# A hand-written order for ScalarE around the S5 output stage: set DMAs behind the next clearing, a sign and four scaling units moved, three scratch rows renamed

## The chip, the cores and the metric

The kernel runs on one core of a Trainium2 chip. The metric is the device time of one execution in microseconds (us). Before the change it is 1008.78 us, the median of three runs (1008.59 to 1009.65). Engines are named as the profile names them: PE is TensorE's matmuls and PEld its weight loads, DVE is VectorE, ACT is ScalarE, POOL is GpSimd, SP is SyncE, which here only issues DMAs. A "q" behind a name (ACTq, SPq) is the engine's queue issuing a DMA.

## The reference

One layer over 1024 latent tokens of width 1024 with a context of 256 tokens, in float32. Depth is 1, so the mixer is the bidirectional S5 state-space model, and only the latent stream is returned.

```python
h_l = modulate(rms_norm(x, norm_mix[i]), m_l[0], m_l[1])      # m_* from SiLU(c) @ ada_w + ada_b
bu = einsum('lgh,gnh->lgn', u, b_bar)                         # 64 groups x 64 complex states, both directions
_, h = associative_scan(combine, (lam_bar, bu))               # h_l = lam_bar h_{l-1} + bu_l, context first
y  = einsum('lgn,ghn->lgh', h, c_mat).real                    # summed over both directions
g  = gelu(y + d_skip * h_l);  x = x + gate * g * sigmoid(g @ w_glu + b_glu)
x  = x + gate2 * swiglu(h2, w1, w3, w2);  out = rms_norm(x, norm_final)
```

## The kernel before, in words

**Chunks.** Tokens are cut into chunks of 8: 32 context chunks and 128 latent chunks. DVE computes the states at the chunk borders one step after another (`scan`): 32 steps of two chunks each up to the middle of the latent stream, then 56 more to its end. What lies inside a chunk is a Toeplitz product. The scan's instructions stand on DVE as one unbroken series; ACT, POOL, PE and SP work beside it on a program of their own.

**Units.** The 64 groups fall into eight units k = 0 to 7 of eight groups, two units to a quarter q = k//2. For each unit PE needs (a) the border states, with the odd chunks of the first half filled in from the even ones, (b) the matrices `CL[q]` that carry a state to the eight tokens of its chunk, and (c) the Toeplitz rows `KQ`.

**The program.** `PROG1` is a string of two-part words that `run` issues in order; each engine sees its own instructions in that order, in program order, and waits by semaphores. Letters: `A` adds more of the conditioning product (`ada`, PE, line 534, with the loads it frees, line 523); `K n` is one half of a quarter's Toeplitz set (`k_mats`: matmuls on lines 845 to 853 into the PSUM tiles `kt` and a second one, two ACT copies on line 856 into `KX`, two DMAs from ACT's queue to DRAM on line 858); `O n` clears the second tile for the next half (`zeros`, ACT copy, line 807); `T n` loads Toeplitz rows back with a shift (`toeplitz`, SP's queue, line 866; `T` number u serves unit u//2); `L` and `G` load the output matrices of a quarter and flip a sign in them (ACT, line 671), `q` sums them (POOL); `C` makes `CL` (POOL products, and for some parts a PE sum with an ACT copy, lines 693 and 694, or an accumulating DMA from POOL, line 696); `f k p` is part p of four of unit k's scaling for the odd chunks (`fill_mul`, four ACT instructions, lines 948 and 949, into a scratch tile `FT[k-2]`); `F k` adds it to the states (`fill_add`, three POOL instructions); `R k` turns the backward states of the first half round (`turned`, ACT copy, line 988, into `HSe[k]`); `P k` is the unit's state product for the first half (PE, line 1008), `X k` its Toeplitz product (PE, line 1032), `Y` the two copies of the result to SBUF (ACT, line 1093). `M` turns the conditioning rows (line 964 copies them out of PSUM).

Then `PROG2` follows: `Z` turns the second half's states (DVE or ACT by `ZEN`), `N k` is the state product of the second half (PE, line 1008 into `pe` tiles), `D` adds it (DVE), `H` the GELU (ACT), `Q 6` and `Q 7` the whole of units 6 and 7, and the GLU begins.

**What holds what.** The PSUM pool behind `P`, `O` and the PE sums has three tiles, so `P k` needs the `Y` copies of the unit before. `PROG1`'s last PSUM tiles are read by `K 7`'s copies; the pool of `PROG2` opens when these and the scan have let go. Every DMA of SP's and ACT's queues takes one of eight completion semaphores in turn, in program order, and its issue waits until the DMA that used the same semaphore before it has landed.

**Rows.** `RA` holds the states; its first 4 KB (`RA` 0 to 4) are context states that are dead after the first scan steps and serve as scratch. `RXc` 0 to 4 is a second scratch, `RC[3]` holds `CL[3]`, whose last 4 KB (12 to 16) are written only by `C33`.

Of the kernel before, what the change touches and what calls it, by code (L numbers as in the profile page):

```python
# [28 lines left out]
MAGIC = 12582912.0  # L29
HOWS = "YPYP EPEP EEEE EPYE"  # L30
ZEN = "VVSVSVSV"
PROG1 = ("A22 G1 B0 A26 A30 C01 O0 C03 q1 A34 K0 O1 L2 A38 A42 C10 C11 K1 O2 G2 A46 A50 C12 C13 f20 f21 A54 K2 O3 f22 f23 A58 T0 T1 T2 T3 q2 C20 R0 R1 K3 L3 C22 F2 A64 M0 P0 R2 f30 f31 X0 Y0 Y1 T4 T5 f32 f33 P1 X1 Y2 Y3 T6 T7 f40 f41 C21 C23 F3 P2 X2 Y4 Y5 R3 G3 M1 q3 K4 f42 f43 C30 P3 K5 X3 Y6 Y7 T8 T9 T10 T11 C31 F4 R4 f50 f51 f52 f53 C32 F5 P4 X4 R5 Y8 Y9 f60 f61 P5 X5 Y10 Y11 C33 f62 f63 K6 K7 f70 f71 f72 f73 F6 F7 T12 T13 T14 T15 w0 l1 M2 m0 w1")
PROG2 = ("Z0 N0 Z1 Z2 D0 Z3 N1 D1 Z4 H0 H1 N2 D2 H2 N3 Z5 D3 H3 N4 D4 z6 z7 I0 J0 I1 J1 H4 N5 D5 I2 J2 H5 I3 J3 W0 W1 W2 W3 x0 x1 x2 x3 Q6 H6 I4 J4 Q7 I5 J5 V1 b0 w20 w21 l1 H7 g03 g13 I6 J6 g23 g05 g15 I7 J7 V2 g26 x10 x11 x12 x13")
GAPS = (5, 6, 6, 6, 6, 6, 6, 8)
LOG2E = 1.4426950408889634
# [7 lines left out]
def s5_ffn_kernel(tc, a, out):  # L43
# [3 lines left out]
    with ctx:  # L47
        ctx.enter_context(tc.manual_schedule())
        sb = ctx.enter_context(tc.tile_pool(name="sb", bufs=1))
        def region(tag, kb, dt=F32):  # L50
            return sb.tile([P, int(kb * 256)], dt, tag=tag, name=tag)

        def view(reg, kb, shape, parts=P):
            off = int(round(kb * 256))
            n = int(np.prod(shape))
            v = reg[:parts, off:off + n]
            if len(shape) > 1:
                names = "abcdef"[:len(shape)]
                v = v.rearrange(f"p ({' '.join(names)}) -> p {' '.join(names)}",
                                **{k: d for k, d in zip(names, shape)})  # L60
            return v

        ENG = {"S": S, "V": V, "E": E}
        R0 = region("r0", 7)
        RA = region("ra", 80.5)
        RU = region("ru", 40)
        RC = [region(f"c{i}", 16) for i in range(4)]
        RXa, RXc = region("rxa", 8), region("rxc", 8)
# [49 lines left out]
        STB = 20.125  # L118
# [60 lines left out]
        def ps_(i):  # L179
            return (LTa, lbt)[i // 8][:, G * (i % 8):G * (i % 8) + G]  # L180

        def t_(i):
            return view(RA, 0.75 + 0.25 * i, [G])
# [31 lines left out]
        k2, k1, p1, dt, k4, kp, pp, sp, cs, pr, lrep, limp, r2p, snp, ta_, tb_ = [ps_(i) for i in range(16)]  # L215
        k3, r1, pw2, be, al, rp, r2, u2, pw3, sn, q1, q2, tc_, td_ = [t_(i) for i in range(14)]
# [449 lines left out]
        def cs_load(q, eng=SY):  # L666
            eng.dma_start(Cs[q][:, 0:2], a["cxy"][:, q])
# [167 lines left out]
        def bb(q, d, ri, a_):  # L835
            return BBn[q // 2][:, ri, d, 8 * (q % 2) + a_]

        def k_mats(q, hq, kts):

            tiles = [(g_, 2 * gi + hq, kts[g_][32 * gi:32 * gi + HC], slice(64 * g_, 64 * g_ + 64), (64 * g_, 32 * gi))  # L840
                     for gi in range(4) for g_ in range(2)]
            for d, c0, c1, ts_ in ((1, 128, 240, slice(7, 0, -1)), (0, 0, 112, slice(6, None, -1))):
                for ri in range(2):
                    for g_, a_, kv, ps, tp in tiles:
                        PE.matmul(kv[:, c0:c1], bb(q, d, ri, a_)[ps], CL[q][ps, ri, d, a_, ts_], start=ri == 0, stop=ri == 1,
                                  tile_position=tp)
            for g_, a_, kv, ps, tp in tiles:
                l0 = 64 * g_ + HC * (tp[1] // 32)
                PE.matmul(kv[:, 112:128], ident[ps, l0:l0 + HC], KD[ps, q, hq], start=True, stop=False, tile_position=tp)
            for d in range(2):  # L850
                for ri in range(2):
                    for g_, a_, kv, ps, tp in tiles:
                        PE.matmul(kv[:, 112:128], bb(q, d, ri, a_)[ps], Cs[q][ps, ri, d, a_], start=False,
                                  stop=d + ri == 2, tile_position=tp)
            for g_ in range(2):
                S.copy(KX[2 * hq + g_], kts[g_])
            for g_ in range(2):
                S.dma_start(KD_[q][:, 2 * hq + g_], KX[2 * hq + g_])

# [77 lines left out]
            while rest:  # L937
                one()

        FT = [view(r, kb, [2, 32, 2, 8]) for r, kb in ((RXc, 0), (RA, STB), (RXc, 0), (RXc, 0), (RA, STB), (RXc, 0))]  # L940

        def fill_mul(k, part):

            ft, e0 = FT[k - 2], 8 * (k % 2)
            st = STQ[k // 2][:, 31:95:2]
# [5 lines left out]
        def fill_add(k):  # L951

            ft, e0 = FT[k - 2], 8 * (k % 2)
            st = STQ[k // 2][:, 32:95:2, :, e0:e0 + 8]
# [79 lines left out]

        scan()
        inner, KO = {}, {}
        HSe = [view(r, kb, [64, 2, 4]) for r, kb in ((RC[3], 14), (RC[3], 12), (RC[3], 14), (RC[3], 12), (RA, 2), (RA, 0))]
        HSl = [view(RA, STB * (i // 3) + 4.125 + 2 * (i % 3), [64, 2, 4]) for i in range(6)]
        HSq = {6: view(RA, 0, [P, 2, 4]), 7: view(RA, STB, [P, 2, 4])}

        def run(prog):


            for w in prog.split():
                op, i = w[0], int(w[1:])
# [4 lines left out]
                elif op == "M":  # L1050
                    mod_cols(i)
                elif op == "K":
                    k_mats(*divmod(i, 2), [kt, KO[i] if i < 4 else pm[:, 0:15 * HC]])
                elif op == "L":
                    cs_load(i, SY if i == 3 else S)
                elif op == "G":
# [8 lines left out]
                elif op == "C":  # L1065
                    q, part = divmod(i, 10)
# [136 lines left out]
        def glu_mm(cq, s):  # L1203
# [14 lines left out]
            return pz  # L1218

        run(PROG1)  # L1220
        psW.__exit__(None, None, None)
        psA.__exit__(None, None, None)
        psE = tc.tile_pool(name="psE", bufs=1, space=bass.MemoryType.PSUM, reuse_waits="tile")
        pE = psE.__enter__()
        for _ in range(4):
            pe8([512])
        run(PROG2)
        W0, GR = W0[0], GR[0]
        X1 = region("c3", 16)
# [93 lines left out]
        for cq in range(2):  # L1323
            for s in range(4):
                k = 4 * cq + s
# [56 lines left out]
        G2 = region("c3", 16, R32)  # L1382
# [420 lines left out]
        for i, (kind, ft, j) in enumerate(seq):  # L1803
# [12 lines left out]
            if kind == "U":  # L1816
# [4 lines left out]
                if (ft, j) in LAST:  # L1821
                    k, h = LAST[ft, j]
# [63 lines left out]
```

## Time and profile before

| | |
|---|---|
| median of three runs | 1008.78 us (1008.59 to 1009.65) |
| the profiled execution, its own time | 1009.95 us |
| its span, first to last instruction | 1008.2 us |
| granted TensorE clock, mean | 0.991 |
| busy: PE, DVE, POOL, ACT | 949.6, 772.8, 746.0, 455.1 us |
| the scan's 88 steps on DVE, last instruction | ends at 216.8 us |
| `P 0`, first matmul on PE | starts at 173.66 us |
| `N 0`, first matmul on PE | starts at 225.28 us |
| from 250 to 330 us | PE busy 20.00 of each 20 us |

Times inside the run are counted from the span's first instruction. In a timeline row the first number is the start, the second the length, and in brackets stands how long the engine was idle before and what ended it. In a table of windows each engine has its busy time in the window with the number of instructions; after POOL stand the granted PE clock (1.00 is full), the mean share of the DMA engines and the GB/s. A busy PE only says that matmuls were in flight.

### The profile page before, as it was taken

What the parts mean: (1) busy time and instruction counts of PE and PEld (TensorE: products, weight loads), DVE (VectorE), ACT (ScalarE), POOL (GpSimd) and SP (SyncE); (2) the same over time, 40 slices, a digit from 0 to 9 for tenths busy, and PEclk for the clock granted to TensorE, in tenths of its full rate; (3) what the DMA queues carried; (4) which work ended last, traced back from release to release, by engine and by line L of the source; (5) the groups of instructions that cost most, each with busy time, mean ns of one, the idle gap of its engine ahead of it and who ended that gap; (6) DMA issues with size and microseconds to landing.
All of it is one profiled execution on the core that took longest, in us unless ns stands there. A gap on an engine that the chain in (4) does not pass through costs nothing. (4 is left out here: it accounts for less than half of the span.)

```text
span 1008.2 us, 17807 instructions
## 1 busy us (share of the span) xinstructions
PE 949.6 (94%) x6604; PEld 748.5 (74%) x6604; DVE 772.8 (77%) x1618; ACT 455.1 (45%) x904; POOL 746.0 (74%) x581
## 2 busy tenths in 40 slices
PE   5987798879999999999999999999999999999996
PEld 1466434758888878778888888888888888888885
DVE  8979999964456777878958677686858677686987
ACT  5488524666434563343243343434243343324337
POOL 5799999764735358979785878777785878777764
PEclk9999998999999999999999999999999999999999
DMA  9765997235521022011212120111212111111205
GB/s 336 282 135 107 298 303 263 70 79 173 180 81 36 0 105 84 12 43 42 73 45 82 42 72 24 62 53 53 73 43 84 42 54 41 54 63 53 73 21 167
DMA packets 48687, 98.39 MB, mean 98 GB/s; under 512 B 4300, under 2 KB 18892, under 8 KB 47320
## 3 DMA queue, kind: packets, MB, share of 16 engines
q1 hardware_dynamic: 43560, 86.91, 26.0%
q0 software_dynamic: 2160, 7.87, 4.2%
q10 hardware_dynamic: 2880, 2.48, 0.8%
q8 instruction: 52, 0.85, 0.3%
q14 instruction: 35, 0.29, 0.1%
HBM read 83.20 MB, written 6.17 MB: 89 GB/s over the span
## 5 line engine op out<-in xcount | busy, mean ns | idle before, releaser
L77 POOL TENSOR_TENSOR c<-rxc,c 128x512 fp32r<-128x512 f32 x127 | 166.0, 1321 | 53.7 <-ACT c L1341 52.9
L1400 PE MATMUL ut<-ra,c 128*128 128x512 f32 x400 | 155.7, 389 | 1.2 <-DVE ra L77 1.2
L1399 PE MATMUL ut<-ra,c 128*128 128x512 f32 x400 | 155.7, 389 | 0.2 <-ACT ra L1341 0.2
L1401 PE MATMUL ut<-ra,c 128*128 128x512 f32 x400 | 155.6, 389 | 0.0
L1341 ACT CAST c<-rxc 128x512 fp32r<-128x512 f32 x128 | 79.1, 622 | 146.7 <-PE xt L1694 53.3
L1694 PE MATMUL xt<-c,c 128*128 128x512 f32 x540 | 129.7, 389 | 0.0
L77 DVE TENSOR_TENSOR ru<-ru,xt 128x1024 f32<-128x1024 f32 x90 | 107.9, 1216 | 13.3 <-PE xt L1694 9.4
L1694 PEld LDWEIGHTS xt<-c,c 128*128 128x128 f32 x540 | 101.4, 188 | 21.0
L77 DVE TENSOR_TENSOR ru<-ut,ru 128x512 f32<-128x512 f32 x98 | 67.2, 686 | 42.6 <-PE ut L1401 37.2
L1400 PEld LDWEIGHTS ut<-ra,c 128*128 128x128 f32 x400 | 75.1, 188 | 17.0 <-POOL rxc L77 1.5
L1399 PEld LDWEIGHTS ut<-ra,c 128*128 128x128 f32 x400 | 75.1, 188 | 16.1 <-ACT ra L1341 0.6
L1401 PEld LDWEIGHTS ut<-ra,c 128*128 128x128 f32 x400 | 75.1, 188 | 15.6
L77 POOL TENSOR_TENSOR rxc<-rxc 128x512 f32<-128x512 f32 (+1 forms) x43 | 64.0, 1487 | 6.9 <-ACT rxc L671 5.3
L77 POOL TENSOR_TENSOR c<-ru,c 128x512 fp32r<-128x512 f32 (+1 forms) x39 | 58.7, 1505 | 10.1 <-ACT c L1341 5.7
L77 POOL TENSOR_TENSOR c<-rw,c 128x512 fp32r<-128x512 f32 (+1 forms) x28 | 37.4, 1336 | 37.3 <-ACT c L1341 37.3
L1399 PE MATMUL ut<-c,c 128*128 128x512 f32 x160 | 62.3, 390 | 0.8 <-DVE rxa L77 0.8
L1401 PE MATMUL ut<-c,c 128*128 128x512 f32 x160 | 62.3, 389 | 0.0
L1400 PE MATMUL ut<-c,c 128*128 128x512 f32 x160 | 62.2, 389 | 0.0
L1694 PE MATMUL ut<-c,c 128*128 128x512 f32 x216 | 51.9, 389 | 0.0
L77 DVE TENSOR_TENSOR ru<-ru,ut 128x512 f32<-128x512 f32 x76 | 47.3, 680 | 0.3
L1694 PEld LDWEIGHTS ut<-c,c 128*128 128x128 f32 x216 | 40.6, 188 | 8.4
L77 DVE TENSOR_TENSOR pe<-pe,ru 128x512 f32<-128x512 f32 x32 | 22.3, 696 | 30.8 <-PE pe L1217 17.1
(462 smaller groups left out, 2432.5 us busy)
## 6 DMA issues: line engine op xcount, KB each, us to landing
c<-in_ada_w SPq DMA_DIRECT2D x46, 256.0 KB, 6.5
rxc<-in_w SPq DMA_DIRECT2D x38, 256.0 KB, 2.9
rxc<-in_w SPq DMA_DIRECT2D x19, 512.0 KB
ru<-in_w SPq DMA_DIRECT2D x11, 512.0 KB
rw<-in_w SPq DMA_DIRECT2D x11, 512.0 KB, 3.6
ra<-in_ada_w SPq DMA_DIRECT2D x10, 512.0 KB, 10.7
c<-c POOLq DMA_DIRECT2D x9, 512.0 KB, 5.7
ra<-in_ada_w SPq DMA_DIRECT2D x18, 256.0 KB, 5.4
```

The costliest lines, as they stand in the source:

```text
L77: eng.tensor_tensor(out=o, in0=x, in1=y, op=op)
L1341: S.copy(o[0], x)
L1399: PE.matmul(pu, wh, bh, start=start, stop=False)
L1400: PE.matmul(pu, wh, bl, start=False, stop=False)
L1401: PE.matmul(pu, wl, bh, start=False, stop=stop)
L1694: PE.matmul(pd, w[:, cs_], b, start=j in (1, 2, 4) and n == 0, stop=n == 2, skip_group_check=j not in (1, 2, 4))
```

## The change

It adds no arithmetic and takes none away. `k_mats` no longer issues its two DMAs; a new word `k` does (`k_rows`), and it stands behind the next `O`. Word by word in `PROG1`: `G3` moves ahead of `f40`; `R2` behind `f30 f31`; unit 5's four parts move ahead of and behind `X3 Y6 Y7`; unit 6's four parts stand together behind `R4`; `Y8 Y9` go ahead of `R5`; unit 7's parts take the place of unit 6's behind `R5` and `Y11`, so none is left behind `C33`. `FT[3]` (unit 5) moves from `RXc` to `RA` 0, and `HSe[4]` from `RA` 2 to `RC[3]` 14.

```diff
-PROG1 = ("A22 G1 B0 A26 A30 C01 O0 C03 q1 A34 K0 O1 L2 A38 A42 C10 C11 K1 O2 G2 A46 A50 C12 C13 f20 f21 A54 K2 O3 f22 f23 A58 T0 T1 T2 T3 q2 C20 R0 R1 K3 L3 C22 F2 A64 M0 P0 R2 f30 f31 X0 Y0 Y1 T4 T5 f32 f33 P1 X1 Y2 Y3 T6 T7 f40 f41 C21 C23 F3 P2 X2 Y4 Y5 R3 G3 M1 q3 K4 f42 f43 C30 P3 K5 X3 Y6 Y7 T8 T9 T10 T11 C31 F4 R4 f50 f51 f52 f53 C32 F5 P4 X4 R5 Y8 Y9 f60 f61 P5 X5 Y10 Y11 C33 f62 f63 K6 K7 f70 f71 f72 f73 F6 F7 T12 T13 T14 T15 w0 l1 M2 m0 w1")
+PROG1 = ("A22 G1 B0 A26 A30 C01 O0 C03 q1 A34 K0 O1 k0 L2 A38 A42 C10 C11 K1 O2 k1 G2 A46 A50 C12 C13 f20 f21 A54 K2 O3 k2 f22 f23 A58 T0 T1 T2 T3 q2 C20 R0 R1 K3 k3 L3 C22 F2 A64 M0 P0 f30 f31 R2 X0 Y0 Y1 T4 T5 f32 f33 P1 X1 Y2 Y3 T6 T7 G3 f40 f41 C21 C23 F3 P2 X2 Y4 Y5 R3 M1 q3 K4 k4 f42 f43 C30 P3 K5 k5 f50 f51 X3 Y6 Y7 f52 f53 T8 T9 T10 T11 C31 F4 R4 f60 f61 f62 f63 C32 F5 P4 X4 Y8 Y9 R5 f70 f71 f72 P5 X5 Y10 Y11 f73 C33 K6 k6 K7 k7 F6 F7 T12 T13 T14 T15 w0 l1 M2 m0 w1")
@@ k_mats
             for g_ in range(2):
                 S.copy(KX[2 * hq + g_], kts[g_])
+
+        def k_rows(q, hq):
             for g_ in range(2):
                 S.dma_start(KD_[q][:, 2 * hq + g_], KX[2 * hq + g_])
@@ fill_mul's scratch
-        FT = [view(r, kb, [2, 32, 2, 8]) for r, kb in ((RXc, 0), (RA, STB), (RXc, 0), (RXc, 0), (RA, STB), (RXc, 0))]
+        FT = [view(r, kb, [2, 32, 2, 8]) for r, kb in ((RXc, 0), (RA, STB), (RXc, 0), (RA, 0), (RA, STB), (RXc, 0))]
@@ turned states
-        HSe = [view(r, kb, [64, 2, 4]) for r, kb in ((RC[3], 14), (RC[3], 12), (RC[3], 14), (RC[3], 12), (RA, 2), (RA, 0))]
+        HSe = [view(r, kb, [64, 2, 4]) for r, kb in ((RC[3], 14), (RC[3], 12), (RC[3], 14), (RC[3], 12), (RC[3], 14), (RA, 0))]
@@ run
                     k_mats(*divmod(i, 2), [kt, KO[i] if i < 4 else pm[:, 0:15 * HC]])
+                elif op == "k":
+                    k_rows(*divmod(i, 2))
```

The orders of PE, DVE, POOL and SP stay as they were; only ACT's rows move, and POOL's and PE's rows read other scratch. In the changed file the lines behind `k_mats` stand two further down, those behind `run`'s new branch four.

ACT at `K 2`, `O 3` and the first rows of `f22`, before and then after (`kt` and `pw` are the two PSUM tiles, `kd` the Toeplitz set in DRAM):

```order
L856 COPY r_60<-kt 128x240
L856 COPY r_60<-pw 128x240
L858 DMA kd_1255<-r_60 128x240 x2
L807 COPY pw<-r_60 128x240
L948 ACTIVATE rxc<-ra,r_60 128x64
```

```order
L856 COPY r_60<-kt 128x240
L856 COPY r_60<-pw 128x240
L807 COPY pw<-r_60 128x240
L860 DMA kd_1255<-r_60 128x240 x2
L950 ACTIVATE rxc<-ra,r_60 128x64
```

The clearing (L807) now stands ahead of the two DMAs instead of behind them.

ACT from `Y 10 Y 11` to the copies of the last Toeplitz halves, before (the eight scalings are `f62 f63`) and then after (the four are `f73`):

```order
L1093 COPY ru<-pw 128x4x8x16 x2
L948 ACTIVATE ra<-ra,r_60 128x64
L949 ACTIVATE ra<-ra,r_60 128x64
L948 ACTIVATE ra<-ra,r_60 128x64
L949 ACTIVATE ra<-ra,r_60 128x64
L948 ACTIVATE ra<-ra,r_60 128x64
L949 ACTIVATE ra<-ra,r_60 128x64
L948 ACTIVATE ra<-ra,r_60 128x64
L949 ACTIVATE ra<-ra,r_60 128x64
L856 COPY r_60<-kt 128x240
L856 COPY r_60<-pm 128x240
L858 DMA kd_1257<-r_60 128x240 x2
```

```order
L1097 COPY ru<-pw 128x4x8x16 x2
L950 ACTIVATE rxc<-ra,r_60 128x64
L951 ACTIVATE rxc<-ra,r_60 128x64
L950 ACTIVATE rxc<-ra,r_60 128x64
L951 ACTIVATE rxc<-ra,r_60 128x64
L856 COPY r_60<-kt 128x240
L856 COPY r_60<-pm 128x240
L860 DMA kd_1257<-r_60 128x240 x2
L856 COPY rw<-kt 128x240
L856 COPY rw<-pm 128x240
L860 DMA kd_1257<-rw 128x240 x2
L990 COPY ra<-ra 128x512 x2
```

Behind the last DMAs the second half's turned states (`Z 2`, `Z 4`, L990 in the changed file, L988 before) now follow at once; before, sixteen scalings of unit 7 stood between.

ACT at the fourth sign, before (behind `Y 4 Y 5` and `R 3`) and after (behind `Y 2 Y 3`):

```order
L1093 COPY ru<-pw 128x4x8x16 x2
L988 COPY c_66<-ra 128x512
L671 ACTIVATE rxc<-rxc 128x256
L972 COPY r_60<-pw 128x4x4 x2
L856 COPY r_60<-kt 128x240
```

```order
L1097 COPY ru<-pw 128x4x8x16 x2
L671 ACTIVATE rxc<-rxc 128x256
L950 ACTIVATE rxc<-ra,r_60 128x64
L951 ACTIVATE rxc<-ra,r_60 128x64
L950 ACTIVATE rxc<-ra,r_60 128x64
```

The sign flip (L671) now stands ahead of `f40 f41` (eight scalings), `Y 4 Y 5` and `R 3`, which were ahead of it.

## The prediction

> **What bounds the kernel now.** I read the windows by stage first, to see where PE, which is in flight 94% of the span, is not. Columns: PE, PEld, DVE, ACT, POOL busy with their counts, PE clock, DMA share, GB/s.
>
> ```profile
> 210.00:230.00 20.00, 13.62 (x483) 12.43 (x487) 8.72 (x43) 11.97 (x37) 9.43 (x8) 0.91 0.14 36
> 230.00:250.00 20.00, 18.84 (x452) 18.00 (x448) 10.39 (x18) 14.24 (x22) 9.44 (x12) 1.00 0.61 186
> 250.00:270.00 20.00, 20.00 (x210) 17.23 (x210) 8.53 (x7) 5.45 (x8) 13.18 (x7) 1.00 0.54 175
> ```
>
> PE lacks 6.4 us between 210 and 230 and 1.2 in the next 20; from 250 on it is full. Whatever brings PE's full stretch forward brings the end forward. So the timeline says which wait ends last there:
>
> ```profile
> 211.84 0.49 PE L1008 MATMUL pw<-c,ra 64*64 64x128 f32 x2 [2.34 <-POOL ra L77]
> 213.65 3.02 PE L1008 MATMUL pw<-c,ra 64*64 64x128 f32 x62 [1.33 <-ACT ru L1093]
> 222.88 0.36 PE L845 MATMUL kt<-c,rxa 64*16 64x112 f32 x2 [1.89 <-ACT r L856]
> 225.28 1.31 PE L1008 MATMUL pe<-c,ra 64*64 64x128 f32 x33 [0.47 <-ACT rw L856]
> 227.45 3.33 PE L1008 MATMUL pe<-c,ra 64*64 64x128 f32 x99 [0.86 <-issue]
> 231.93 4.35 PE L1008 MATMUL pe<-c,ra 64*64 64x128 f32 x131 [1.16 <-ACT ra L988]
> 216.78 0.76 DVE L990 COPY ra<-ra 128x512 f32<-128x512 f32 x2
> 228.82 1.29 DVE L77 TENSOR_TENSOR ru<-pe,ru 128x512 f32<-128x512 f32 x2 [11.27 <-PE pe L1008]
> ```
>
> These are `P 5` (two rows), `K 7`, `N 0`, `N 1`, `N 2`; then DVE's turned states `Z 0 Z 1`, right behind the scan. DVE is done with the scan at 216.78 and then idles 11.27 us for PE. So the scan is not the bound: `N 0` could start at 217.2 (half of the 0.76) and starts at 225.28. Those **8.1 us are the most** that an earlier `N 0` can give; the 1.16 us ahead of `N 2` (ACT's `Z 2`) come on top. PE is held by ACT, directly or through POOL:
>
> ```profile
> 204.60 0.61 ACT L988 COPY ra<-ra 128x512 f32<-128x512 f32 x1
> 209.54 0.40 ACT L949 ACTIVATE rxc<-ra,r 128x64 f32<-128x64 f32 x1
> 212.50 0.62 ACT L988 COPY ra<-ra 128x512 f32<-128x512 f32 x1 [2.56 <-POOL ra L77]
> 213.02 1.07 ACT L1093 COPY ru<-pw 128x512 f32<-128x512 f32 x2
> 219.19 1.07 ACT L1093 COPY ru<-pw 128x512 f32<-128x512 f32 x2 [2.72 <-PE pw L1032]
> 222.49 0.34 ACT L856 COPY r<-kt 128x240 f32<-128x240 f32 x1
> 225.25 1.22 ACTq L858 DMA_DIRECT2D kd<-rw  x2
> 231.28 1.12 ACT L988 COPY ra<-ra 128x512 f32<-128x512 f32 x2
> 209.74 2.73 POOL L77 TENSOR_TENSOR ra<-ra,rxc 128x512 f32<-128x512 f32 x3 [2.35 <-ACT rxc L948]
> 214.53 2.39 POOL L77 TENSOR_TENSOR c<-c,rw 128x1024 f32<-128x1024 f32 x1
> ```
>
> From `R 4` (ends 205.2) to the last of unit 5's sixteen scalings (ends 209.94) a scaling costs 0.30 us. Then POOL adds (`F 5`, 209.74), ACT turns (`R 5`, 212.50), copies `Y 8 Y 9` (213.02), and only then PE gets the bulk of `P 5`. Behind `Y 10 Y 11` (219.19) eight more scalings hold `K 6`'s copies until 222.49, and sixteen more hold `Z 2` until 231.28.
>
> **The change, part by part.**
>
> *The sets' DMAs behind the clearing.* Three of the four clearings were not waited for by PE. The fourth was:
>
> ```profile
> 166.38 0.97 ACTq L858 DMA_DIRECT2D kd<-r  x2
> 167.39 0.36 ACT L807 COPY pw<-r 128x240 f32<-128x240 f32 x1 [3.42 <-DMA c<-in_ada_w]
> 167.81 0.36 PE L845 MATMUL pw<-c,c 64*16 64x112 f32 x1 [3.26 <-ACT pw L807]
> 168.00:170.00 2.00, 2.00 (x139) 1.97 (x125) 2.00 (x13) 2.00 (x8) 1.50 (x2) 0.50 0.62 165
> 173.66 0.39 PE L1008 MATMUL pw<-c,ra 64*64 64x128 f32 x2
> 164.26 0.80 SPq L523 DMA_DIRECT2D ra<-in_ada_w  x2
> ra<-in_ada_w SPq DMA_DIRECT2D x10, 256.0 KB, 5.0
> 170.06 1.13 ACT L988 COPY c<-ra 128x512 f32<-128x512 f32 x2
> 173.81 0.59 ACT L964 COPY ra<-pm 128x512 f32<-128x512 f32 x1 [2.11 <-PE pm L534]
> ```
>
> `K 2`'s copies end at 167.39 − 3.42 = 163.97; the DMAs then wait for a semaphore that an `in_ada_w` load still holds, and `O 3` with `K 3` waits behind them. PE idles 3.26 us and comes back at half clock (0.50 in 168 to 170), so `K 3` and `A 64` last until 173.7 and `P 0` starts at 173.66. Now `O 3` runs at 163.9 and `K 3` from 164.3 to 166.0 (1.7 us: `K 6` runs from `X 5`'s end near 219.3 to 222.88 − 1.89). `A 64` waits for its last load, issued at 164.7 and 5.0 us on its way: done near 170.0. The DMAs still hold `f22` until 167.4 instead of 167.7, so `R 0`, which stood at 170.06, comes at 169.75 and `P 0`'s bulk at **170.3: 3.3 us earlier**. `k0`, `k1`, `k3` cost nothing: ACT issues the same two DMAs one 0.36 us copy later, and their readers `T` go out microseconds later (below).
>
> *The middle of the program.* A `P` costs 2.3 and an `X` 2.05 us at full clock:
>
> ```profile
> 177.40 7.00 SPq L866 DMA_DIRECT2D ra<-kd  x4
> 205.26 2.26 PE L1008 MATMUL pw<-c,ra 64*64 64x128 f32 x60 [0.77 <-ACT ra L988]
> 175.86 2.05 PE L1032 MATMUL pw<-ra,ru 128*128 128x128 f32 x16
> 178.92 1.05 ACT L1093 COPY ru<-pw 128x512 f32<-128x512 f32 x2
> 196.77 0.17 PE L853 MATMUL pm<-rw,rxa 64*16 64x16 f32 x1 [1.92 <-issue]
> 196.93 3.13 PE L1032 MATMUL pw<-ra,ru 128*128 128x128 f32 x16
> 199.66 1.07 ACT L1093 COPY ru<-pw 128x512 f32<-128x512 f32 x2 [2.02 <-PE pw L1032]
> 198.00:200.00 2.00, 2.00 (x11) 2.00 (x11) 2.00 (x13) 0.34 (x1) 2.00 (x2) 0.50 0.38 123
> ```
>
> `X 0` ends at 174.7. ACT meanwhile does `K 3`'s copies, `M 0` (172.0; `A 64` no longer holds it to 173.81), `f30 f31` (2.4) and `R 2` (0.5), and reaches `Y 0` at 175.4, not 178.92. `R 2` behind `f30 f31` waits for nothing: `P 0`, whose row it reuses, is over. `P 1` needs `Y 0`: `X 1` ends at 180.2, `P 2` and `X 2` at 185 (their `T` loads go out from 177.40 on, as before), `K 4` at 187.4, `P 3` at 189.8, `K 5` with the 1.92 us stall that the profile puts down to nothing at 193.4, `X 3` at 3.13 (half clock again) at 196.6. Unit 5's first two parts (2.4) stand ahead of `Y 6` now, behind `K 5`'s copies and DMAs: ACT is free at 197.2, so `Y 6` comes at 197.2, not 199.66, 0.6 later than it could. Next `f52 f53` 2.4, two PE-sum copies and `R 4` at 201.6, not 204.60. **3.0 of the 3.3 us survive.**
>
> *The sign.*
>
> ```profile
> 189.78 0.43 ACT L671 ACTIVATE rxc<-rxc 128x256 f32<-128x256 f32 x1
> 190.29 0.73 POOL L77 TENSOR_TENSOR rxc<-rxc 128x256 f32<-128x256 f32 x1 [5.35 <-ACT rxc L671]
> ```
>
> POOL idles 5.35 us for `G 3`. Behind `Y 2 Y 3` it comes near 181.3; POOL is then still in `C 23` and `F 3` (free at 190.29 − 5.35 = 184.94), so POOL's whole series moves forward by 5.3. Alone that is worth nothing to PE, since `F 5` waits for ACT (2.35). It pays with the next part, as `F 5` then finds POOL free.
>
> *Unit 5 in other rows, earlier; units 6 and 7 earlier.* Unit 5's scratch in `RA` 0 lets it start without waiting for `F 4` to leave `RXc`. Its last scaling ends at 200.6 instead of 209.94; `F 5` (2.73) runs behind POOL's `C 32`, which ends 206.50 + 0.88 − 5.3 before and so near 202, until 204.8. `P 4` and `X 4` after `R 4` end at 206.5. Unit 6's sixteen (4.7) stand behind `R 4` and end at 206.9: **`Y 8` at 206.9 instead of 213.02, `R 5` at 208.0 instead of 212.50, the bulk of `P 5` at 208.5 instead of 213.65: 5.2 us.** `X 5` ends 4.3 us on (full clock) or 5.8 (3.02 + 2.8, as in the trace): 212.8 to 214.3. `Y 10 Y 11` and four scalings of unit 7 (1.07 + 1.2) put `K 6`'s copies at 215.1 to 216.6 instead of 222.49. From them to `N 0` it is 225.28 − 222.49 = 2.8: **`N 0` at 217.9 to 219.4**, 0.7 behind the scan's floor or more.
>
> `HSe[4]` in `RC[3]` makes `C 33`'s product wait for `P 4` (204.4). `C 33` takes 4.5 (to 216.92 in the trace, from 212.4), so it ends near 209.3; `K 6` needs it at 212.8. The cover is 3.5 us; only what `P 4` loses beyond would cost. `F 6` and `F 7` end before 220 on an idle POOL.
>
> *Behind `N 0`.* ACT issues `k7`'s DMAs (1.22) and does `Z 2` at once, so `N 2` follows `N 1`: 5.5 us after `N 0` (230.78 − 225.28), at 223.4 to 224.9 instead of 231.93. **Sum: 7.0 to 8.5 us; I take 7.8.** `T12` to `T15` and the GLU's loads stand on SP's queue behind `k7` and move with it by 6 to 7 us, and PE needs `T12` only at `Q 6`, so they stay hidden; all later work hangs on PE.
>
> The profiled execution took 1009.95, 1.17 above the median of the runs: 1002.2 for one like it and **1001.0 us** against 1008.78.
>
> [...]
>
> **The rivals.** *The first 3.3 us are lost* (20%): the loads of `A 64` come later, or PE idles in pieces between them and stays at half clock through `P 0` and `X 0`, as in 168 to 170. For it: PE has only six matmuls between 166 and 170. Then `Y 6` comes at 200.7, later than before, behind `f50 f51`; `R 4` 205.2, `Y 8` 210.4, `P 5` 212.1, `N 0` 221.5 to 223.0, `N 2` 227.0 to 228.5: 4.2 us, 1004.6.
>
> *Nothing at the end* (5%): a load or POOL takes PE's place behind `N 0` and 1008.8 stays. Against it: PE's 20.00 of 20 from 250, with DMA at 0.54 of its time.
>
> *Slower* (5%): PE's rows of small matmuls are fed no faster than now. The gaps of 1.92 and 0.86 with "issue" behind them stand in such rows, and the change packs `K 3`, `K 4`, `K 6` and `K 7` closer. A stall costs 1.92, and 1.08 for the half clock behind it (3.13 − 2.05): 3.0. Two leave a gain; from three on (9.0 against 7.8) it is slower: 1010.0. Against it: `K 6` and `N 2` to `Q 7` run as dense as that without one.
>
> **How the numbers follow.** The forecast has 68%, with its own range 999.4 (8.5 and the 0.86 gap gone) to 1002.6; 2% lie below. The range for 8 in 10 takes in most of the first rival: 999.0 to 1005.0. Below 0.2% (2 us) a measurement of this kernel cannot be told from no change; so faster 0.90, same 0.05, slower 0.05.
>
> **What would show it.** Right: `K 3`'s first matmul near 164.3 with no half clock behind it; `P 0` near 170.3; POOL's sum of the fourth sign near 185; `F 5` with no wait for ACT; `N 0` near 218 and DVE's idle ahead of it down from 11.27 to some 4 us; no wait ahead of `N 2`; the span after 250 as long as before. Wrong: an `N 0` beyond 222, new "issue" gaps, or PE idle behind 250 that was not there.

## The result, and the profile after

The changed kernel takes 1003.34 us (median of five runs, 1001.83 to 1006.10), the kernel before 1009.44 (1008.59 to 1011.98): ratio 0.9939, 95% interval 0.9916 to 0.9962, so 6.1 us faster and at least 3.8. The profiled execution of the changed kernel took 1001.83 us, with a span of 1000.0 against 1008.2 before. The executions of either kernel lie 3 to 4 us apart here and up to 7 us in the later runs; how that bears on the numbers is taken up below.

The windows of the profile after, by stage, with the columns of the table before:

```profile
210.00:230.00 20.00, 17.67 (x670) 16.63 (x664) 14.37 (x54) 12.14 (x27) 6.14 (x9) 1.00 0.34 88
230.00:250.00 20.00, 20.00 (x394) 18.56 (x389) 8.03 (x12) 8.79 (x14) 11.62 (x10) 1.00 0.44 154
250.00:270.00 20.00, 20.00 (x100) 16.50 (x99) 9.15 (x10) 9.14 (x13) 14.93 (x7) 1.00 0.66 224
```

PE had 13.62 and 18.84 us busy in the first two windows; it has 17.67 and 20.00 now, 5.2 us more, and the clock in the first is 1.00 where it was 0.91. The timeline shows the same steps as before the change, some now in other rows. PE first (`P 5` in two rows, `K 7`, the first 33 matmuls of `N 0`, and the rest of `N 0` with everything up to the GELU's first transposes as one row), then DVE, ACT and POOL:

```profile
208.25 0.48 PE L1010 MATMUL pw<-c,ra 64*64 64x128 f32 x2 [0.58 <-ACT ru L1097]
209.25 2.25 PE L1010 MATMUL pw<-c,ra 64*64 64x128 f32 x60 [0.52 <-ACT ra L990]
217.36 0.25 PE L845 MATMUL kt<-c,rxa 64*16 64x112 f32 x1 [0.42 <-issue]
218.92 1.31 PE L1010 MATMUL pe<-c,ra 64*64 64x128 f32 x33 [0.47 <-ACT rw L856]
220.93 9.28 PE L1010 MATMUL pe<-c,ra 64*64 64x128 f32 x287 [0.70 <-issue]
217.24 1.32 DVE L992 COPY ra<-ra 128x512 f32<-128x512 f32 x2
222.30 1.29 DVE L77 TENSOR_TENSOR ru<-pe,ru 128x512 f32<-128x512 f32 x2 [3.75 <-PE pe L1010]
207.63 1.04 ACT L1097 COPY ru<-pw 128x512 f32<-128x512 f32 x2
208.57 0.62 ACT L990 COPY ra<-ra 128x512 f32<-128x512 f32 x1
215.43 0.35 ACT L856 COPY r<-kt 128x240 f32<-128x240 f32 x1
219.99 1.14 ACT L990 COPY ra<-ra 128x512 f32<-128x512 f32 x2 [0.86 <-ACT rw L856]
184.35 0.73 POOL L77 TENSOR_TENSOR rxc<-rxc 128x256 f32<-128x256 f32 x1
201.22 3.08 POOL L77 TENSOR_TENSOR ra<-ra 128x512 f32<-128x512 f32 x3
205.42 2.03 POOL L77 TENSOR_TENSOR c<-rxc,rxa 128x1024 f32<-128x1024 f32 x1 [1.12 <-PE pw L1010]
```

`N 0` starts at 218.92 instead of 225.28, DVE's idle ahead of `D 0` is 3.75 us instead of 11.27, and no row stands between 220.93 and 230.21 in which PE waits, so the 1.16 us ahead of `N 2` are gone. The 0.70 us with "issue" stand inside `N 0`, as the 0.86 us did before: a state product has 64 matmuls, and the row ahead of the gap holds 33 of them. The prediction, and the expectations of e3 and e9, put that gap into `N 1`; it lies in `N 0`, so `D 0` waits for it. At the front, `O 3` runs ahead of the two DMAs, but `K 3` has a gap of its own:

```profile
162.84 0.38 ACT L807 COPY pw<-r 128x240 f32<-128x240 f32 x1
164.59 1.40 ACTq L860 DMA_DIRECT2D kd<-r  x2
166.03 0.41 ACT L950 ACTIVATE rxc<-ra,r 128x64 f32<-128x64 f32 x1 [2.81 <-DMA c<-in_ada_w]
167.11 0.19 PE L853 MATMUL kt<-rxc,c 64*16 64x16 f32 x1 [2.48 <-issue]
193.57 0.18 PE L853 MATMUL pm<-rw,rxa 64*16 64x16 f32 x1 [2.46 <-issue]
193.75 3.78 PE L1034 MATMUL pw<-ra,ru 128*128 128x128 f32 x16
```

The clearing no longer waits; the DMAs and the scalings behind them do. PE's two gaps of 2.5 us with "issue" behind them, in `K 3` and in `K 5`, are what the rest of the study turns on.

### The profile page after: what moved, and what is told of

Its sections match the earlier page's. It is cut to its first block, busy times and chain, and to the rows that moved or that the text cites. A ratio compares the mean times of both kernels' runs of the same rounds, so it can differ in the third digit from the quotient of the medians.

```text
span 1000.0 us, 17808 instructions
## 1 busy us (share of the span) xinstructions
PE 949.0 (95%) x6604; PEld 749.1 (75%) x6604; DVE 772.9 (77%) x1618; ACT 454.7 (45%) x904; POOL 746.3 (75%) x581
## 3 DMA queue, kind: packets, MB, share of 16 engines
q10 hardware_dynamic: 2880, 2.48, 0.8%
```

## The experiments

**A clock for comparing single profiles.** Executions of one kernel differ by up to 2.6 us before the first moved word is reached: `bb_turn` (L827), which stands ahead of all of them, starts at 127.75 in the first profile of the changed kernel and at 130.34 in its second. The second and third profiles are e4 and e11 for the changed kernel, e8 and e12 for the kernel before. So I count from the start of DVE's `Z 0`, which follows the scan at once and waits for nothing else, to `D 0`, DVE's first addition behind `N 0`, and from there to the end. Both are rows of DVE's timeline; the first two here are of the changed kernel's third profile, the last two of the third profile of the kernel before:

```profile
217.28 0.76 DVE L992 COPY ra<-ra 128x512 f32<-128x512 f32 x2
220.98 1.29 DVE L77 TENSOR_TENSOR ru<-pe,ru 128x512 f32<-128x512 f32 x2 [2.94 <-PE pe L1010]
```

```profile
217.08 0.76 DVE L990 COPY ra<-ra 128x512 f32<-128x512 f32 x2
228.00 1.29 DVE L77 TENSOR_TENSOR ru<-pe,ru 128x512 f32<-128x512 f32 x2 [10.16 <-PE pe L1008]
```

All profiles, read in this way (us; the last two columns are the timed runs against the kernel before, on the same chip):

| kernel | Z 0 starts | Z 0 to D 0 | D 0 to end | ratio | interval |
|---|---|---|---|---|---|
| before | 216.8, 217.2, 217.1 | 12.0, 11.9, 10.9 | 779.4, 779.4, 778.7 | 1 | |
| changed | 217.2, 219.9, 217.3 | 5.1, 6.0, 3.7 | 777.7, 777.6, 777.6 | 0.9939; 0.9938 | 0.9916 to 0.9962; 0.9914 to 0.9961 |
| e1, sets alone | 219.0 | 9.2 | 779.4 | 0.9978 | 0.9962 to 0.9993 |
| e2, no sets | 216.7 | 6.7 | 779.7 | 0.9936 | 0.9915 to 0.9958 |
| e3, 128 PE instructions more | 218.8 | 8.6 | 777.9 | 0.9940 | 0.9917 to 0.9963 |
| e5, no sign | 216.9 | 4.0 | 777.7 | 0.9945 | 0.9927 to 0.9962 |
| e6, unit 7 late | 216.9 | 7.5 | 778.9 | 0.9952 | 0.9936 to 0.9967 |
| e7, before with R 2 moved | 216.7 | 11.9 | 779.7 | 0.9986 | 0.9972 to 1.0001 |
| e9, tail | 217.1 | 5.5 | 778.0 | 0.9924 | 0.9907 to 0.9941 |
| e10, tail and k2 | 218.6 | 4.2 | 777.8 | 0.9929 | 0.9905 to 0.9953 |

By the means of three, the change takes 6.7 us out of the stretch from `Z 0` to `D 0` (11.6 to 4.9) and 1.5 out of what follows (779.2 to 777.6): **8.2 us**, with 1 to 2.3 us between profiles of one kernel.

### The sets' DMAs alone, and all but them

e1 is the kernel before with only the words `k` (`... K0 O1 k0 ... K2 O3 k2 ...`), e2 the changed kernel with them back:

```diff
-K0 O1 k0 ... K1 O2 k1 ... K2 O3 k2
+K0 k0 O1 ... K1 k1 O2 ... K2 k2 O3
```

> The kernel before with only the sets' DMAs behind the next clearing; signs, units and scratch rows as before. Theory of the sum: P 0 starts at 170.3 instead of 173.66, 3.0 of the 3.3 us survive to R 4 (201.6), and nothing behind R 4 takes them, so N 0 starts near 222.3 instead of 225.28 and the time is 1009.4 - 3.0 = 1006.4. Rival: the gain is lost in the middle, at K 5 and X 3 or at F 5, and N 0 stays at 225: 1009.4. Both expect the idle 2.5 us inside K 3 that the changed kernel shows, since K 3 then runs at once.

> The changed kernel with the sets' DMAs back in their old place, ahead of the clearings; all else as changed. Theory of the sum: P 0 back at 173.7, Y 6 near 200.7, Y 8 near 210.4, N 0 at 221.5 to 223, so 4.2 us of the gain are left: 1005.2. Rival: the new order of the units alone carries the end, because PE makes up the lateness between X 3 and P 4, where it waits for ACT: N 0 near 219 and the time that of the changed kernel, 1002 to 1003.3.

e1 took 1007.21 us against 1010.02: 2.2 us by the ratio (0.7 to 3.8), with `D 0` 2.4 us nearer to `Z 0`. The theory of the sum said 3.0 and holds; that the gain is lost in the middle does not. The idle stretch that both texts expected inside `K 3` stood in `K 2` this time (2.66 us). e2 took 1003.78, as much as the changed kernel in the same runs (1003.76), where the sum said 1005.2. The medians side with the rival, but the interval reaches from 4.2 to 8.6 us of gain and so just takes in the sum's 4.2 as well. In its profile `O 3` waits as before the change, yet `D 0` comes only 1.7 us later than in the changed kernel's mean:

```profile
165.30 1.29 ACTq L860 DMA_DIRECT2D kd<-r  x2
166.64 0.36 ACT L807 COPY pw<-r 128x240 f32<-128x240 f32 x1 [3.19 <-DMA c<-in_ada_w]
```

Counted from `Z 0`, `P 0` starts 44.0 us ahead of it in e2 and 47.1, 46.6 and 48.1 ahead in the three profiles of the changed kernel: 3.3 us on average. At `P 4`'s bulk the difference is 1.8, and it stays so to `N 0`. So the first part's gain exists, almost half of it is gone by `P 4`, and on top of the units less than 2 us of it are left at `D 0`, which these intervals cannot tell from nothing. The first 1.0 us goes between `P 0` and `K 4` (14.0 us in e2, 15.0 on average in the changed kernel): PE waits there for `Y 0` ahead of `P 1`, 0.70 and 1.08 us in the second and third profile of the changed kernel, and not at all in e2.

Behind `D 0` e2 is 2.1 us longer than the changed kernel. One row in `N 4` accounts for it:

```profile
232.20 1.27 PE L1010 MATMUL pe<-c,ra 64*64 64x128 f32 x31 [1.97 <-issue]
```

At that place no profile of the changed kernel has a gap. Counted from `Z 0` to the end, e2's profile therefore keeps 4.4 of the 8.2 us, and 6.4 without this gap; the timed runs keep 6.4.

### What "issue" is

PE's instructions, counted from 0 in the order of their start, have gaps with "issue" at the 2713th, 2969th, 3989th, 4245th, 5011th and 5267th in the changed kernel's first profile: in pairs of 256. The page lists 52 packets on an instruction queue; PE has 13208 instructions (matmuls and weight loads), 254 for each packet:

```profile
PE 949.0 (95%) x6604; PEld 749.1 (75%) x6604; DVE 772.9 (77%) x1618; ACT 454.7 (45%) x904; POOL 746.3 (75%) x581
...
q8 instruction: 52, 0.85, 0.3%
```

e3 puts 128 more instructions of PE ahead of all this:

```diff
-        def k_mats(q, hq, kts):
+        def k_mats(q, hq, kts, pad=0):
+            for g_, a_, kv, ps, tp in tiles * pad:
+                PE.matmul(kv[:, 112:128], ident[ps, 0:HC], KD[ps, q, hq], start=True, stop=True, tile_position=tp)
@@ run
-                    k_mats(*divmod(i, 2), [kt, KO[i] if i < 4 else pm[:, 0:15 * HC]])
+                    k_mats(*divmod(i, 2), [kt, KO[i] if i < 4 else pm[:, 0:15 * HC]], 4 * (i == 0))
```

> The changed kernel with 128 more PE instructions (32 small matmuls into columns that K 0 overwrites) ahead of K 0, near 143 us, where PE waits for loads behind it. Theory of the feed: PE's 13208 instructions come in 52 packets, 254 each, and the gaps with issue stand 256 instructions apart (the 2969th and the 4245th, in K 3 and K 5; the 5011th and the 5267th, in K 7 and N 1). Every such edge now falls 128 instructions earlier in the program: no gap over 1 us in K 3 any more, at most 1 us in K 5, X 3 back from 3.78 towards 2.05 us, and new gaps of 2 to 2.5 us at the end of K 6 or in K 7. Up to X 3 it runs 2 to 3 us ahead of the changed kernel, at K 7 it gives 2 to 3 back: N 0 between 218 and 221, 1002 to 1005. Rival: the gaps belong to these matmuls (a load, a wait that the profile does not show): they stay at the same matmuls with 2.5 us, N 0 at 218.9, and the time is the changed kernel's plus at most 0.8.

> The changed kernel itself once more, on the same chip as the other three, to compare them with. Theory of the sum: 1001.0 to 1003.3. If the gaps of the feed vary from execution to execution, its times spread over 4 us as they did, and the gaps of this profile differ in length from the first one's; if they are fixed, K 3 and K 5 show 2.5 us again.

PE's timeline of e3, at the gaps (ahead of `K 1`, in `K 3`, `P 3`, `K 5`, `K 7`):

```profile
151.14 0.59 PE L534 MATMUL pm<-c,r 128*2 128x512 f32 x2 [2.10 <-issue]
168.58 0.25 PE L847 MATMUL kt<-c,c 64*16 64x112 f32 x1 [1.10 <-issue]
194.79 0.37 PE L1012 MATMUL pw<-c,ra 64*64 64x128 f32 x1 [1.61 <-issue]
198.52 0.19 PE L851 MATMUL pm<-r 64*16 64x16 f32 x1 [0.74 <-issue]
224.09 0.19 PE L855 MATMUL pm<-rxc,rxa 64*16 64x16 f32 x1 [0.92 <-issue]
```

The last four stand at the 2969th, 3991st, 4247th and 5269th instruction: the same numbers to within 2, on other matmuls, 128 earlier in the program. The gap in `K 3` has moved from its L853 rows to its first ones (L847 here), that of `K 5`'s first rows is in `P 3`, and that of `N 0` is in `K 7`. So the gaps go with the count of instructions, not with a matmul or a load, and the rival falls. The transfers of the instruction queue, which are in the traces too, agree: each carries 16384 bytes, and all nine gaps with "issue" on PE's timelines in the first profiles of the two kernels end 2.2 to 2.5 us after one of these transfers has started. The six of the changed kernel follow the 10th, 11th, 15th, 16th, 19th and 20th transfer, one transfer for each 255 to 256 instructions between them. That PE waits there for its next packet of instructions is my reading of these counts and times, not a row of a trace; I call this supply the feed.

The expected sizes were half right: `K 5`'s gap fell to 0.74 and `X 3` ran at a clock of 1.00 (190 to 200; eleven of its sixteen matmuls in 1.49 us), but `P 3` got a new gap of 1.61, `K 3`'s stayed over 1, and none in `K 6` or `K 7` reached 2. The time did not move (0.9940 against 0.9938).

In the profile `N 0` starts at 224.97, outside the expected 218 to 221, and `D 0` is 3.7 us later than in the changed kernel's mean. That was not foreseen. e3 has one more gap, 2.10 us at number 2203 near 151 us, ahead of `K 1`, but of the lateness only 1.3 us are there at `P 0`. Another 3.1 come between `P 0` and `K 4`: PE waits for `Y 0`, which ACT reaches 3.0 us later than in the changed kernel, and then runs at a granted clock of 0.56 and 0.59 (180 to 184); 0.7 are made up later.

```profile
180.12 0.48 PE L1012 MATMUL pw<-c,ra 64*64 64x128 f32 x1 [1.94 <-ACT ru L1099]
```

Why ACT is late there, and whether the extra gap set it off, is not shown. The profiled execution is also e3's slowest (1008.15 us, median 1004.88), so its lateness need not be that of the others.

The second and third profiles of the changed kernel have the gaps at the same instructions (the 2713th, 2969th, 4245th, 5011th and 5267th are in all three), with other lengths: 1.66 in `K 3` in both, 1.92 and 2.46 in `K 5`. So in these three executions the place is the same and the length differs, by up to 0.8 us in `K 3`.

### The sign back in its place

```diff
-T6 T7 G3 f40 f41 C21 C23 F3 P2 X2 Y4 Y5 R3 M1 q3
+T6 T7 f40 f41 C21 C23 F3 P2 X2 Y4 Y5 R3 G3 M1 q3
```

> The changed kernel with the fourth sign back behind Y 4 Y 5 and R 3; all else as changed. Theory of the sum: POOL's series depends on the sign, F 5 finds POOL busy until it is 2 us late, R 5, P 5 and N 0 are 2 us later: N 0 about 4 us behind the scan's end instead of 1.7 and 2.4, 1005.8 where the changed kernel has 1003.8. Rival: ACT is itself 5 us earlier at Y 4, so the sign stands near 186 and POOL's sum only 1.8 us later than in the changed kernel; F 5 ends near 206, 2 us before ACT comes to R 5 (208.6), and nothing is later: 1003.8.

1002.02 us against 1009.33 (0.9945). POOL and ACT of e5, at the sum of the fourth sign, at `F 5` and at `R 5`:

```profile
185.82 0.73 POOL L77 TENSOR_TENSOR rxc<-rxc 128x256 f32<-128x256 f32 x1 [1.82 <-ACT rxc L671]
202.66 3.09 POOL L77 TENSOR_TENSOR ra<-ra 128x512 f32<-128x512 f32 x3
207.34 0.63 ACT L990 COPY ra<-ra 128x512 f32<-128x512 f32 x1
```

POOL's wait is back with 1.82 us, not 5.35, and `F 5` is done 1.6 us ahead of `R 5`, which waits for nothing. The rival holds: with the rest of the change in place the sign brings `N 0` nothing. The rows decide this; the interval alone (0.9927 to 0.9962) would also take in the 2 us of the sum.

### Unit 7 behind K 7 again

```diff
-R5 f70 f71 f72 P5 X5 Y10 Y11 f73 C33 K6 k6 K7 k7 F6
+R5 P5 X5 Y10 Y11 C33 K6 k6 K7 k7 f70 f71 f72 f73 F6
```

> The changed kernel with unit 7's four parts behind K 7 again, as before; all else as changed. Theory of the sum: K 6's copies wait for PE and come no earlier (215.4), N 0 stays at 218.9 (1.7 to 2.4 us behind the scan's end); but sixteen scalings, 4.7 us, stand ahead of Z 2, which ends near 225.8, so N 2 waits about 2 us where it now waits for nothing: 1005.8 against 1003.8. Rival: the 1.2 us of wait that stood ahead of N 2 are all that the earlier place of unit 7 took away, or F 7 and Q 7 hide it: at most 1.2 us, 1003.8 to 1005.0.

1004.50 us against 1009.33 (0.9952). ACT's `Z 2`, and PE at `N 2`:

```profile
226.65 1.13 ACT L990 COPY ra<-ra 128x512 f32<-128x512 f32 x2
227.31 4.98 PE L1010 MATMUL pe<-c,ra 64*64 64x128 f32 x152 [1.05 <-ACT ra L990]
```

The wait ahead of `N 2` is back with 1.05 us and the stretch from `D 0` to the end is 1.3 longer. Of the two sizes the rival's (at most 1.2) is right and the sum's (2) too large, because the feed's gap in `N 0`, 0.97 us here, makes PE late for `N 2` anyway: 1.05 and 0.97 are the sum's 2. `D 0` is 2.5 us later than in the changed kernel's mean; this execution has 2.75 us of "issue" in `K 3` and starts `P 0` 43.5 us ahead of `Z 0`, so that is not unit 7's.

### R 2 alone

```diff
-P0 R2 f30 f31 X0
+P0 f30 f31 R2 X0
```

> The kernel before with nothing changed but R 2, which stands behind f30 f31 instead of ahead of them. Theory of the sum: R 2's place costs nothing and brings nothing, N 0 stays 8.5 us behind the scan's end, 1009.4 to 1010.0. Rival, from the run without the sets' move, where P 2 came 1.2 us sooner behind P 1 than before: ahead of P 0's end R 2 holds ACT 1.6 us, Y 0 comes 1.0 us behind the end of X 0 and PE idles 1.2 us ahead of the bulk of P 1; without that N 0 is 1.2 us earlier, 7.3 us behind the scan's end, and the time 1008.8.

1007.94 us against 1009.33; the interval (0.9972 to 1.0001) holds both theories. The profile shows both halves of an answer: from `P 0`'s start to `K 4`'s it is 14.0 us instead of 15.2 in each of the three profiles before, so the 1.2 us ahead of `P 1` are won; from `K 4` to `X 3` it is 9.5 instead of 8.0 to 8.7, with three gaps, of which this is the last:

```profile
196.84 0.18 PE L853 MATMUL pm<-rw,rxa 64*16 64x16 f32 x1 [2.46 <-issue]
```

`Z 0` to `D 0` is 11.9 us, as before. In this execution the feed took back what `R 2` had won.

### A changed tail, and k2 later

Two versions aim at what is left: e9 by ACT's order at the end, e10 by the same and by `k2` behind the scalings that it holds up.

```diff
-R4 f60 f61 f62 f63 C32 F5 P4 X4 Y8 Y9 R5 f70 f71 f72 P5 X5 Y10 Y11 f73 C33 K6 k6 K7
+R4 f60 f61 f62 C32 F5 P4 X4 R5 Y8 Y9 f63 f70 f71 P5 X5 Y10 Y11 C33 K6 k6 f72 f73 K7
```

and in e10 also

```diff
-K2 O3 k2 f22 f23
+K2 O3 f22 f23 k2
```

> The changed kernel with ACT's order at its end changed further: R 5 ahead of Y 8 Y 9, f63 behind them, f72 and f73 behind the copies of K 6. Theory of the sum: Y 8 starts at the end of X 4, 207.3, not at 207.63, and the bulk of P 5 at 208.0 to 208.4 instead of 209.25, since R 5 is done by then; K 6's copies at 214.2 instead of 215.43, so N 0 is 0.9 to 1.2 us earlier: 0.5 to 1.3 us behind the scan's end instead of 1.7 and 2.4, 1002.8 against 1003.8. Rival, the feed: the packet edge in K 7 comes 3.2 us behind the one in K 6 (214.15, 217.36), and that in N 1 3.6 behind it, whatever ACT does; K 6 starts 0.9 earlier, K 7's gap grows from 0.42 to about 1, and N 0 gains 0.5 at most.

> The run before this one, and k2's DMAs behind f22 f23 as well, so that their wait for a semaphore holds no scaling any more (2.81 us of ACT's time ahead of f22 in the changed kernel). Theory of the sum: R 0 and R 1, K 3's copies and M 0 come up to 2 us earlier; P 0 gains 0 to 1 (it also needs A 64), Y 0 up to 1, and N 0 another 0 to 1: 1002.3. Rival: nothing, since P 0 waits for A 64 and K 5's gap takes what is left, as the whole of the sets' part brought 0 to 1.6 on top of the units: equal to the run before this one.

e9 took 1001.99 us and e10 1002.31 against 1009.87. PE of e9 at `P 5`, `K 7` and `N 0`, and ACT at `K 6`'s copies:

```profile
208.34 2.79 PE L1010 MATMUL pw<-c,ra 64*64 64x128 f32 x64
217.37 0.25 PE L845 MATMUL kt<-c,rxa 64*16 64x112 f32 x1 [1.07 <-issue]
218.95 1.31 PE L1010 MATMUL pe<-c,ra 64*64 64x128 f32 x33 [0.49 <-ACT rw L856]
214.78 0.36 ACT L856 COPY r<-kt 128x240 f32<-128x240 f32 x1 [0.78 <-PE pm L853]
```

`P 5` is one row now with no wait in it and `K 6`'s copies come 0.65 earlier, but the gap in `K 7` ends at 217.37, where it ended at 217.36 in the changed kernel, and `N 0` comes at 218.95: the gap grew from 0.42 to 1.07. The rival holds. e10's `Z 0` to `D 0`, 4.2, is inside the 3.7 to 6.0 of the changed kernel, and its ratio is e9's within 0.0005, as its rival has it. By the timed runs both are the fastest versions measured, 1 to 1.5 us below the changed kernel by the ratios; their intervals overlap with its own, so that is not shown.

### Third profiles

> The changed kernel, a third profile. N 0 stands 1.7 and 2.4 us behind the scan's end in the first two, the end 782.8 and 783.6 us behind it. The same again, 1.5 to 2.6 and 782.5 to 784, if the stretch from the scan on is steady and the executions differ in their first 220 us; anything outside would put part of the spread into the stretch of the change.

> The kernel before, a third profile. N 0 stands 8.5 and 8.8 us behind the scan's end in the first two, the end 791.4 and 791.3 us behind it. The same again if the stretch is steady, so that the change's gain there is 8 us; if it is 2 us less in some executions, that is why the medians differ by 6.1 and 6.3 us and not by 8.

Both fell outside what I gave them (`N 0` 0.4 us behind `Z 0`'s start, and 6.6): the stretch varies by up to 2.3 us. In the third profile of the kernel before, `N 0` itself ran at half clock (0.50 from 224 to 228), so `N 0` starts 2.0 us nearer to `Z 0` than in the first two and `D 0` only 1.1. In the changed kernel's third profile `N 0` waits for the scan's turned states and no longer for ACT, the floor that the prediction named:

```profile
217.70 1.32 PE L1010 MATMUL pe<-c,ra 64*64 64x128 f32 x33 [0.47 <-DVE ra L992]
```

They do not close the account. The stretch from the scan on is 8.2 us shorter by three profiles each, the medians differ by 6.1 to 6.3 in 13 runs. The intervals reach 8.5 and 8.7 us, so some of it may be chance. From `bb_turn` to the end the means of three differ by 8.0, so nothing is lost between `bb_turn` and `Z 0`. Part may lie ahead of that: `Z 0` starts at 218.6 to 219.9 in four of the eleven profiles with an edit in them and at 216.7 to 217.3 in the other seven and in all three before. In three of the four `bb_turn` starts at 129.5 or later already, before any moved word, so no way from the change to it is known. It stays open.

## Why the prediction was right, step by step

**The bound.** Right. PE's full stretch hung on `N 0`, `N 0` on ACT's chain, and the scan was the floor, which one profile of three reached. Of the 8.1 us named as the most, 6.5 were used by the means of three: `N 0` starts 1.5 us behind `Z 0` instead of 8.0.

**The first 3.3 us.** The size was right, on the scan's clock too (3.0 us at `P 0` by the means of three), the way was wrong. The step "`K 3` from 164.3 to 166.0" and the sign "no half clock behind it" failed: PE began `K 3` at once, stood 2.48 us with "issue" ahead of the 2969th instruction, and the clock fell all the same, as two windows of the changed kernel say:

```profile
168.00:170.00 2.00, 2.00 (x12) 0.11 (x4) 2.00 (x13) 2.00 (x6) 2.00 (x2) 0.60 0.60 180
170.00:172.00 2.00, 2.00 (x39) 1.83 (x41) 2.00 (x13) 1.18 (x5) 1.92 (x3) 0.54 0.76 235
```

That `P 0` came at 170.17, as predicted, was luck. The forecast hung it on the last load of `A 64`, issued at 164.7 and 5.0 us on its way. That load was issued at 163.66 and landed 4.7 us later, near 168.3, and `A 64`, which starts at 167.50 right behind `K 3`, hardly waited for it. What held `P 0` was the gap and then the lower clock in `A 64`'s last four matmuls: they took 1.88 us (168.35 to 170.2, clock 0.60 from 168 to 170), the eight before them 1.04. The load came earlier than priced and `K 3` ended later, by about as much.

**The middle.** "3.0 of the 3.3 us survive" was some 0.4 to 0.8 too much: `R 4` started at 202.35 instead of the 201.6 predicted, and `P 4`'s bulk is 2.6 us earlier on the scan's clock. The step that failed is `K 5`'s stall, taken over from the old trace as 1.92 and `X 3` as 3.13: they were 0.59 + 2.46 and 3.78. `R 2`'s place, which I counted together with the sets, is a gain of its own of 1.2 us ahead of `P 1` where the sets stay (e7); with the sets moved, the wait ahead of `P 1` was back with 0.70 and 1.08 us in two of three profiles.

**The sign.** Half wrong. POOL's sum of the fourth sign ran at 184.35 without a wait (predicted near 185), and `F 5` at 201.22 without one for ACT. But "it pays with the next part" failed: without it POOL is 1.4 to 1.5 us later and still done 1.6 us ahead of the reader (e5). I had compared with POOL's old times, not with those that ACT's own earlier arrival gives.

**Units 5, 6 and 7.** Each time was in the right order, the first three 0.6 to 0.8 later than predicted, the others inside their ranges: `Y 8` 207.63 (206.9), `R 5` 208.57 (208.0), `P 5`'s bulk 209.25 (208.5), `K 6`'s copies 215.43 (215.1 to 216.6), `N 0` 218.92 (217.9 to 219.4), `N 2` behind its wait for ACT 223.97 (223.4 to 224.9). `C 33` did wait for `P 4`, 1.12 us, and was done at 209.90, 3.5 us ahead of `K 6`: the cover held. The 1.16 us ahead of `N 2` came in full, with a little more. Units 5 and 6 and the place of `Y 8 Y 9`, the largest part of the sum, have no run of their own; that they carry the gain rests on these rows and on e2.

**The clock.** The two ends of the sum, 8.5 and 7.0 us, had `X 5` end 4.3 us behind the start of `P 5`'s bulk, at full clock, or 5.8, as in the trace before the change. It ended 4.2 behind it: `P 5`, with 0.58 and 0.52 us idle ahead of its two rows, ran its bulk in 2.25 us and `X 5`, from 211.43, took 2.05, at a clock of 1.00 (210 to 220). But the runs show why a row from one execution is no price: the windows of the kernel before, of the changed kernel's first profile and of its second, 190 to 210, show the slow stretch in different places.

```profile
190.00:200.00 10.00, 7.82 (x287) 7.27 (x277) 10.00 (x58) 4.42 (x16) 9.56 (x6) 0.88 0.17 53
200.00:210.00 10.00, 8.73 (x89) 5.70 (x87) 10.00 (x58) 7.17 (x21) 7.27 (x7) 0.95 0.63 146
```

```profile
190.00:200.00 10.00, 7.54 (x139) 5.88 (x123) 10.00 (x59) 6.78 (x23) 9.92 (x7) 0.66 0.19 52
200.00:210.00 10.00, 8.13 (x113) 6.08 (x115) 10.00 (x59) 9.49 (x28) 8.42 (x8) 1.00 0.65 134
```

```profile
190.00:200.00 10.00, 7.75 (x259) 6.40 (x247) 10.00 (x58) 5.65 (x19) 9.84 (x8) 1.00 0.17 53
200.00:210.00 10.00, 8.01 (x80) 5.67 (x79) 10.00 (x58) 10.00 (x31) 7.73 (x7) 0.83 0.66 132
```

In the second profile of the changed kernel `X 3` runs at a clock of 1.00 (190 to 200) behind a gap of 1.92 us. `P 4`, some 9 us later, is the slow one: from the start of its bulk to `X 4` it is 3.51 us (205.37 to 208.88), where the first profile has 2.19 (203.01 to 205.20).

**The rivals.** *The first 3.3 us are lost* was priced at 4.2 us of gain left. Without them e2 kept 6.4 by the timed runs (4.2 to 8.6) and 4.4 in its one profile, where 1.97 us are the gap in `N 4`. The failed step is "then `Y 6` comes at 200.7", which carried the lateness on in full: in e2's profile `Y 6` comes at 198.79 and `N 0` at 219.99, not at 221.5 to 223.0. *Slower through "issue" gaps* named the right place and the wrong size: new gaps did come, in `K 3` and `K 7` (2.48 and 0.42 us), where no profile of the kernel before has any, though the prediction had named them as a sign of being wrong. They were partly under waits that were there before, and they did not undo the gain.

**The number.** 1001.0 was taken as the median before less 7.8. The stretch of the change gave 8.2; the median fell by 6.1, to 1003.34. That lies inside the range for 8 in 10, but outside the forecast's own 999.4 to 1002.6, and it is nearer to the first rival's 1004.6 than to 1001.0. So the time alone would not tell the two apart; the rows do. What was too large is the step from a profiled stretch to the median, by about 2 us if that is more than chance, and its cause is the open point above.

## What to carry to other kernels

Before pricing a move of ACT's or POOL's work, ask what PE will do with the time: here rows of tiny matmuls ran 288 instructions in 1.7 us where no gap fell among them, and stood up to 2.48 us with "issue" in the changed kernel's first profile where one did, so a wait taken away in front of them came back in part as such a gap. Price a moved instruction against the times the rest of the change will produce, not against the old trace: the sign was worth 5 us of POOL's idle time there and nothing here. And where executions differ by several us, compare stretches from an event that the change cannot move, in more than one profile of each kernel.

## What the runs showed of the hardware

- PE's "issue" gaps stand at the same counts of instructions, 256 apart in pairs, in the changed kernel and, to within 2, in e3, where other matmuls lie there. The rows of the changed kernel at 217.36 and 220.93, and of e9 at 217.37 and 221.21, put the ends of two gaps 3.6 and 3.8 us apart although PE had waited in between: 256 instructions in that time, about 70 per us. One half of a Toeplitz set is 288 instructions, and `K 0`, `K 1` and `K 4` of the changed kernel run through it in 1.7 us each, with no gap. The nine gaps of the first profiles of both kernels end 2.2 to 2.5 us after a transfer of 16384 bytes on the instruction queue has started. The gaps of the changed kernel's first profile are 0.42 (`K 7`) to 2.48 us long (`K 3`); that in `K 3` had 2.48, 1.66 and 1.66 us in its three profiles. A step freed of a wait can get a gap instead: `K 3` waited 3.26 us for `O 3` before the change, and stood 2.48 us with "issue" after it.
- Behind a gap of 1.92 us in `K 5` the clock fell in the next `X 3` in one execution and later in another, with PE's order the same: the kernel before ran `X 3` in 3.13 us from 196.93 (clock 0.92 from 196 to 198, 0.50 from 198 to 200); the second profile of the changed kernel had 1.00 from 190 to 200, with `X 3`, and 0.83 from 200 to 210, with `P 4`. What sets the moment, no run here shows.
